# RWKV-7 chain outputs batched over four chunks, pairwise products grouped apart from transposes, low-rank rest weights padded to all rows

## The chip, the cores and the metric

The kernel runs on one core of a Trainium2 chip. The metric is the device time of one execution in microseconds (us). Three runs of the kernel before took 931.61, 930.42 and 931.18 us, with a median of 931.18 us.

## What is computed

One layer of a hybrid block over 512 tokens of width 1024: a norm, one wide input projection, two branches beside each other (RWKV-7 time mixing and a chunked Gated DeltaNet), sigmoid gates that merge them, an output projection, a gated MLP with a causal convolution, and a last norm. The change lies in the RWKV-7 branch, of 8 heads with 64 features:

```python
w_log = -softplus(-(w0 + tanh(wl) @ w2)) - 0.5      # wl, al: 64 wide, low rank
a = sigmoid(a0 + al @ a2)
kk = l2norm(heads(k * k_k)); k = k * (1 + (a - 1) * k_a)
def step(S, inp):                                   # per token and head
    sa = einsum('bhvk,bhk->bhv', S, a_t)
    S = S * w_t + sa * b_t + v_t * k_t              # outer products
    y = einsum('bhvk,bhk->bhv', S, r_t)
    return S, y
```

The kernel computes the scan in 8 chunks of 64 tokens: the state goes from chunk to chunk, and the outputs `y` of a chunk need the state at its start and the solved values inside it.

## The kernel before

Features lie on partitions, the 512 tokens in the free dimension. Nearly all of the work is dense products: a unit of 128 output features takes its weights from memory (`unit`, L148), splits them into two fp32r parts `hi` (ScalarE, L161) and `lo` (VectorE or GpSimd, L163), and multiplies both by the activations in three passes (`mm3`, L169: L176, L177, L179; 24 products of 128x512 for an input unit). The string `ORDER` (L26) is the order in which stages are written; a scheduler then makes one fixed instruction list for each engine from it, in which dense products of later units fill the places where a stage waits. Each engine works through its list strictly in order.

The parts that the change touches:

- `first_tiles` (L256) loads the low-rank weights once and leaves their rest part `ll` in one tile, the decay's in partitions 0 to 63 and the rate's in 64 to 127 (L289, L290). `rwkv_prep` (L422), called once for each of four head pairs (R0 to R3 in `ORDER`), multiplies them: L438 and L474 over all 128 rows of the array, L439 and L475 over 64.
- `rwkv_prep` ends with two halves of four chunks. For each chunk there are two products over 64 rows (L504, L505) and a transpose over all rows (L506), written in turns.
- `rwkv_chain` (L585), called for head pairs 0 and 1 and again for 2 and 3 (c0 and c1 in `ORDER`), runs 8 chunks. A chunk has these steps: L618 and L619 (PE, `128*64`), the copy `Z` (VectorE, L621), L624 (PE, `64*64`), the scaling of the result by VectorE and ScalarE in turns (L626, L627), L630 and L631 (PE, `128*64`), and the new state (VectorE, L637, or L640 in the first chunk), from which the next chunk starts. Beside this loop stand 8 output products a chunk: L642 and L644 (`128*64`), L643 and L645 (`64*64`). ScalarE takes the outputs away once in four chunks (L648).

`128*64`, `64*64`, `64*128` and `128*128` are the array's forms, rows by columns in use, as the profile writes them. A product of fp32 operands is two passes, that is two rows of the profile; a product of fp32r operands is one.

```python
for i, hp in enumerate(hps):
    nc.tensor.matmul(py[lo, i, c4, :], se[:, i, 0, :], R[hp]["ase"][:, c, 1, :], start=True, stop=False)
    nc.tensor.matmul(py[lo, i, c4, :], se[lo, i, 1, :], R[hp]["ntb"][lo, c, 1, :], start=False, stop=True)
    nc.tensor.matmul(py[hi, i, c4, :], so[:, i, 0, :], R[hp]["aso"][:, c, 1, :], start=True, stop=False)
    nc.tensor.matmul(py[hi, i, c4, :], so[hi, i, 1, :], R[hp]["ntb"][hi, c, 1, :], start=False, stop=True)
```

Of the kernel before, what the change touches and what calls it, by code (L numbers as in the profile page):

```python
# [16 lines left out]
T = 512  # L17
# [16 lines left out]
# columns of the per-feature parameter array  # L34
# [9 lines left out]
# columns of the shape-only constant array  # L44
# [49 lines left out]
class Body:  # L94
# [27 lines left out]
    # elementwise work without PSUM operands that GpSimd takes over from VectorE  # L122
# [13 lines left out]
    # work of the second stream takes its temporaries from its own slots  # L136
# [31 lines left out]
    # ps (+)= W^T A with both operands in two parts; act(k) gives the k-th activation tile's parts  # L168
# [35 lines left out]
    # running sum of squares over feature tiles, then 1/sqrt(mean) on all partitions  # L204
# [17 lines left out]
    def run(self):  # L222
# [11 lines left out]
        self.ll = c.tile([128, 512], F32R, name="lora_l")  # L234
# [19 lines left out]
    # the input, its norm, and the first projections, which take the gained but not yet normalised  # L254
    # input and are scaled per token afterwards
    def first_tiles(self, xp):  # L256
# [6 lines left out]
        # zero products keep the array's clock up until the first operands are there  # L263
# [22 lines left out]
        # the low-rank weights stand twice, on either half of the partitions, beside both parts of their input  # L286
        nc.scalar.activation(self.lh, raw, AF.Copy)
        lo, hi = slice(0, 64), slice(64, 128)
        for s, o in ((lo, 0), (hi, 512)):  # L289
            self.on("q").tensor_tensor(out=self.ll[s], in0=raw[s, o:o + 512], in1=self.lh[s, o:o + 512].bitcast(F32), op=ALU.subtract)  # L290
# [48 lines left out]
    # token shift mix of one dense tile  # L339
# [13 lines left out]
    def mixing(self, first):  # L353
# [37 lines left out]
        # the first branch's projection, in the inverse's tiles  # L391
# [7 lines left out]
    # one tile of the branch gates; without a place for it on chip it goes out and comes back for the merge  # L399
# [22 lines left out]
    def rwkv_prep(self, hp, first=None):  # L422
# [12 lines left out]
        # decay  # L435
# [3 lines left out]
        nc.tensor.matmul(ps, self.ll[0:64, fs], self.xw[0:64], start=False, stop=True)  # L439
# [13 lines left out]
        # key norm: one over the squared norm, per token and head on partitions  # L453
# [18 lines left out]
        # in-context rate and replacement key  # L472
        ps = self.bank()
        nc.tensor.matmul(ps, self.lh[:, 512 + hp * 128:640 + hp * 128], self.xa, start=True, stop=False)  # L474
        nc.tensor.matmul(ps, self.ll[64:128, fs], self.xa[64:128], start=False, stop=True)  # L475
# [15 lines left out]
        # bonus  # L491
# [4 lines left out]
        # pairwise products inside a chunk  # L496
        rwm = self.con("rwm")
        for h in range(2):
            pe, po, pt = self.bank(), self.bank(), self.bank()
            for c in range(4):  # L500
                o = slice(c * 128, c * 128 + 128)
                cc = 4 * h + c
                bk = bkh[h][:, c, :, :].rearrange("p s t -> p (s t)")
                nc.tensor.matmul(pe[:, o], bk[0:64], ase[0:64, cc].rearrange("p s t -> p (s t)"), start=True, stop=True)  # L504
                nc.tensor.matmul(po[:, o], bk[64:128], aso[64:128, cc].rearrange("p s t -> p (s t)"), start=True, stop=True)  # L505
                nc.tensor.transpose(pt[:, o], bk, self.con("ident"))  # L506
# [14 lines left out]
    # transposed inverses of G unit triangular 32x32 blocks per 32 partitions, Y = I + N^T Y: a block goes  # L521
    # to J partitions, each with every J-th of its columns
# [62 lines left out]
    def rwkv_chain(self, g, R):  # L585
# [3 lines left out]
        # the values lose their mean over a head's features here: the recurrence is linear in each of  # L589
        # them, so the output that the group norm takes has none either  # L590
        cent = self.con("cent")

        def suv():
            return [self.mp.tile([128, 2, 2, 64], F32, tag=f"SUV{x}", name=self.nm("SUV"), bufs=2) for x in "eo"]
# [3 lines left out]
        nc.gpsimd.memset(so[hi, :, 0, :], 0.0)  # L598
        for c in range(8):
            if c % 4 == 0:  # L600
                pv = self.bank().rearrange("p (c i t) -> p c i t", c=4, i=2)
                py = self.bank().rearrange("p (i c t) -> p i c t", c=4, i=2)
# [5 lines left out]
            c4 = c % 4  # L608
            for tl, s in ((se, hi), (so, lo)):
                nc.scalar.activation(tl[s], pv[s, c4].unsqueeze(2).broadcast_to([64, 2, 2, 64]), AF.Copy)  # L610
            ws = self.mp.tile([128, 2, 64], F32, tag="WS", name=self.nm("WS"), bufs=2)
            if c:
# [28 lines left out]
            for i, hp in enumerate(hps):  # L641
                nc.tensor.matmul(py[lo, i, c4, :], se[:, i, 0, :], R[hp]["ase"][:, c, 1, :], start=True, stop=False)  # L642
                nc.tensor.matmul(py[lo, i, c4, :], se[lo, i, 1, :], R[hp]["ntb"][lo, c, 1, :], start=False, stop=True)  # L643
                nc.tensor.matmul(py[hi, i, c4, :], so[:, i, 0, :], R[hp]["aso"][:, c, 1, :], start=True, stop=False)  # L644
                nc.tensor.matmul(py[hi, i, c4, :], so[hi, i, 1, :], R[hp]["ntb"][hi, c, 1, :], start=False, stop=True)  # L645
            if c4 == 3:
                for i, hp in enumerate(hps):
                    nc.scalar.activation(R[hp]["v"][:, (c - 3) * 64:(c + 1) * 64].rearrange("p (c t) -> p c t", c=4),  # L648
                                         py[:, i], AF.Copy)
# [88 lines left out]
    def gdn_prep(self, h):  # L738
# [6 lines left out]
        # twice the silu of the convolved query, key and value; the norms come in as factors per token:  # L745
        # the key's through beta and the value, the query's through the guard of the output's norm
# [307 lines left out]
```

## Time and profile before

| what | value |
|---|---|
| median of three runs | 931.18 us |
| span of the profiled execution | 929.5 us; what lies around it in the median run is 1.7 us |
| mean granted TensorE clock | 0.993 of full |
| busy: PE, VectorE (DVE), ScalarE (ACT), GpSimd (POOL) | 897.3, 599.5, 466.0, 193.5 us |
| instructions on PE | 4925 matmuls, 4925 weight loads |

A PE row's duration is the time from its start to its modelled end, and one product starts before the one ahead of it has ended. What a product costs is therefore read as the distance from its start to the next start, not as its duration.

### The profile page before, as it was taken

The page shows a single profiled execution, that of the slowest core. Times are in us where ns is not written, and L with a number is a line of the kernel's source. Part 1 is how long each engine was busy: PE and PEld are TensorE (multiplying, and loading weights), DVE is VectorE, ACT ScalarE, POOL GpSimd, SP SyncE. Part 2 cuts the span into 40 slices and gives each one's busy share as a digit, 9 for nine tenths or more (in the row PEclk, how much of TensorE's full clock was granted, in tenths as well). Part 3 has the DMA queues.
Part 4 walks back from the last instruction along what each step waited for, and adds up shares of the span by engine and source line. Part 5 has one row for each costly group of instructions (what it writes and reads, how often), then busy time and mean ns, then how long its engine had stood idle before and what let it go on. Part 6 is the DMA issues. An engine that isn't in the chain of part 4 may idle for free.

```text
span 929.5 us, 13149 instructions
## 1 busy us (share of the span) xinstructions
PE 897.3 (97%) x4925; PEld 686.4 (74%) x4925; DVE 599.5 (65%) x1156; ACT 466.0 (50%) x887; POOL 193.5 (21%) x180
## 2 busy tenths in 40 slices
PE   8999998999999989999999999999999999999995
PEld 5767676665766676666787788888888888888885
DVE  6799797762888995664458445887666666412125
ACT  7744456557643766548533445444444444423233
POOL 1331123101211121101122221222222222222221
PEclk8999999999999999999999999999999999999998
DMA  6422121121112220115343332333322333233334
GB/s 230 136 81 71 57 79 56 47 68 34 59 46 79 68 69 24 57 58 178 106 133 139 95 109 69 109 95 97 106 92 90 95 104 97 80 107 84 104 95 139
DMA packets 28737, 84.76 MB, mean 91 GB/s; under 512 B 3200, under 2 KB 5376, under 8 KB 28672
## 3 DMA queue, kind: packets, MB, share of 16 engines
q1 hardware_dynamic: 28672, 83.91, 28.7%
q8 instruction: 39, 0.64, 0.3%
q14 instruction: 26, 0.21, 0.1%
HBM read 78.13 MB, written 5.77 MB: 90 GB/s over the span
## 4 chain that ended last, share of the span: by engine, by line
PE 75%; DVE 17%; ACT 4%; issue 2%; DMA 1%; POOL 1%; SPq 0%; DVEq 0%; POOLq 0%; ACTq 0%
PE D L179 20%; PE D L176 19%; PE D L177 19%; DVE R L510 2%; PE A L176 1%; PE A L177 1%; PE A L179 1%; DVE P L732 1%; DVE lo L163 1%; DVE invN L539 1%; DVE invY L541 1%; DVE BK L490 1%; DMA raw<-w_in 1%; PE B L643 1%; PE B L644 1%
## 5 line engine op out<-in xcount | busy, mean ns | idle before, releaser
L163 POOL TENSOR_TENSOR lo<-raw,hi 128x512 fp32r<-128x512 f32 x133 | 178.3, 1341 | 662.6 <-ACT hi L161 653.9
L161 ACT ACTIVATE hi<-raw 128x512 fp32r<-128x512 f32 (+1 forms) x266 | 164.7, 621 | 243.1 <-PE D L179 183.1
L176 PE MATMUL D<-uh,lo 128*128 128x512 f32 (+1 forms) x456 | 184.9, 407 | 2.3 <-ACT uh L200 1.9
L177 PE MATMUL D<-uh,hi 128*128 128x512 f32 (+1 forms) x456 | 184.4, 405 | 0.0
L163 DVE TENSOR_TENSOR lo<-raw,hi 128x512 fp32r<-128x512 f32 (+1 forms) x133 | 93.1, 700 | 80.8 <-ACT hi L161 80.3
L179 PE MATMUL D<-ul,hi 128*128 128x512 f32 (+1 forms) x456 | 138.7, 406 | 0.4 <-DVE ul L198 0.4
L176 PE MATMUL D<-u2h,lo 128*128 128x512 f32 x352 | 138.2, 393 | 0.0
L177 PE MATMUL D<-u2h,hi 128*128 128x512 f32 x352 | 138.0, 392 | 0.0
L176 PEld LDWEIGHTS D<-uh,lo 128*128 128x128 f32 x456 | 85.7, 188 | 23.1 <-ACT uh L200 2.4
L177 PEld LDWEIGHTS D<-uh,hi 128*128 128x128 f32 x456 | 85.9, 188 | 18.8 <-issue 1.4
L179 PEld LDWEIGHTS D<-ul,hi 128*128 128x128 f32 x456 | 82.5, 188 | 19.6 <-issue 1.0
L179 PE MATMUL D<-u2l,hi 128*128 128x512 f32 x352 | 94.6, 391 | 0.0
L957 DVE SCALAR_TENSOR_TENSOR P<-T,vecs,P 128x511 f32<-128x511 f32 x88 | 77.4, 880 | 7.4 <-ACT P L955 2.2
L176 PEld LDWEIGHTS D<-u2h,lo 128*128 128x128 f32 x352 | 66.1, 188 | 15.1 <-issue 0.4
L179 PEld LDWEIGHTS D<-u2l,hi 128*128 128x128 f32 x352 | 66.1, 188 | 14.5
L177 PEld LDWEIGHTS D<-u2h,hi 128*128 128x128 f32 x352 | 66.1, 188 | 14.3 <-issue 0.2
L954 DVE TENSOR_TENSOR T<-D,acc 128x512 f32<-128x512 f32 x44 | 30.3, 688 | 41.0 <-PE D L179 37.0
L177 PE MATMUL D<-ah,hi 128*128 128x512 f32 (+1 forms) x126 | 45.2, 366 | 0.0
L176 PE MATMUL D<-ah,lo 128*128 128x512 f32 (+1 forms) x126 | 45.1, 366 | 0.0
L955 ACT ACTIVATE P<-T,vecs 128x512 f32<-128x512 f32 x44 | 31.8, 722 | 8.8 <-DVE T L954 6.0
L539 DVE TENSOR_TENSOR invN<-invA,invY 128x60 f32<-128x60 f32 (+24 forms) x124 | 33.6, 271 | 2.8
L541 DVE TENSOR_TENSOR invY<-invY,invN 128x60 f32<-128x60 f32 (+24 forms) x124 | 33.0, 266 | 2.7
(345 smaller groups left out, 1329.6 us busy)
## 6 DMA issues: line engine op xcount, KB each, us to landing
raw<-w_in SPq DMA_DIRECT2D x44, 512.0 KB, 3.6
raw<-ffn_up SPq DMA_DIRECT2D x44, 512.0 KB, 3.6
raw<-ffn_down SPq DMA_DIRECT2D x18, 512.0 KB, 3.6
raw<-w_out SPq DMA_DIRECT2D x8, 512.0 KB, 3.7
spill<-T SPq DMA_DIRECT2D x14, 256.0 KB, 2.0
R<-spill SPq DMA_DIRECT2D x14, 256.0 KB, 5.3
raw<-ffn_down SPq DMA_DIRECT2D x9, 384.0 KB, 3.1
xin<-xT SPq DMA_DIRECT2D x8, 256.0 KB, 5.4
```

The source lines that it names most:

```text
L161: nc.scalar.activation(hi[:, 0:w], raw[:, o:o + w], AF.Copy)
L163: self.on(str(self.halves % 4)).tensor_tensor(out=lo[:, 0:w], in0=raw[:, o:o + w], in1=hi[:, 0:w].bitcast(F32), op=ALU.subtract)
L176: nc.tensor.matmul(ps, wl[:, w[k]], x[k][0], start=(first and i == 0 and k == 0), stop=False)
L177: nc.tensor.matmul(ps, wh[:, w[k]], x[k][0], start=False, stop=False)
L179: nc.tensor.matmul(ps, wh[:, w[k]], x[k][1], start=False, stop=(last and i == len(parts) - 1 and k == n - 1))
L490: self.on("c").tensor_tensor(out=bkh[h][s, :, sk, :], in0=q(K, s, h), in1=q(em, s, h), op=ALU.mult)
L510: nc.vector.tensor_tensor(out=tl[s, w].rearrange("p c s t -> p c (s t)"), in0=ps[s, :].rearrange("p (c t) -> p c t", c=4), in1=rwm[s].unsq ...
L539: nc.vector.tensor_tensor(out=w, in0=rows[:, t, 0:t].unsqueeze(2).broadcast_to([128, t, n]), in1=Ym[:, t, c:G].unsqueeze(1).broadcast_to([ ...
L541: nc.vector.tensor_tensor(out=Ym[:, 0:t, c:G], in0=Ym[:, 0:t, c:G], in1=w, op=ALU.add)
L954: nc.vector.tensor_tensor(out=h, in0=ps, in1=self.acc2, op=ALU.mult)
L955: nc.scalar.activation(cv, h, AF.Copy, scale=w(2))
L957: nc.vector.scalar_tensor_tensor(out=cv[:, sh:], in0=h[:, 0:T - sh], scalar=w(2 - sh), in1=cv[:, sh:], op0=ALU.mult, op1=ALU.add)
```

## The change

Three edits, and room made for them. The outputs of a chain are no longer issued chunk by chunk: the states of four chunks are kept (`SUV` gets six buffers in place of two), and all outputs of chunks 0 to 3 are issued after chunk 4, those of chunks 4 to 7 after chunk 7; first all 16 products of form `128*64`, then all 16 of form `64*64`, low and high half in turns. In the preparation the four transposes of a half follow its eight products. The low-rank rest weights become two tiles of 128 rows, with zeros in the other half, so that their products use all rows. In the last chunk the scaled state `ws`, which nothing reads there, is no longer made. The scratch for dynamic DMA is set to 1024. The other lines of the diff are removed comments.

```diff
-        self.ll = c.tile([128, 512], F32R, name="lora_l")
+        self.ll = [c.tile([128, 512], F32R, name=f"lora_l{i}") for i in range(2)]
...
-        for s, o in ((lo, 0), (hi, 512)):
-            self.on("q").tensor_tensor(out=self.ll[s], in0=raw[s, o:o + 512], in1=self.lh[s, o:o + 512].bitcast(F32), op=ALU.subtract)
+        for ll, s, z, o in ((self.ll[0], lo, hi, 0), (self.ll[1], hi, lo, 512)):
+            nc.gpsimd.memset(ll[z].bitcast(F32), 0.0)
+            self.on("q").tensor_tensor(out=ll[s], in0=raw[s, o:o + 512], in1=self.lh[s, o:o + 512].bitcast(F32), op=ALU.subtract)
...
-        nc.tensor.matmul(ps, self.ll[0:64, fs], self.xw[0:64], start=False, stop=True)
+        nc.tensor.matmul(ps, self.ll[0][:, fs], self.xw, start=False, stop=True)
...
-        nc.tensor.matmul(ps, self.ll[64:128, fs], self.xa[64:128], start=False, stop=True)
+        nc.tensor.matmul(ps, self.ll[1][:, fs], self.xa, start=False, stop=True)
...
-                nc.tensor.transpose(pt[:, o], bk, self.con("ident"))
+            for c in range(4):
+                nc.tensor.transpose(pt[:, c * 128:c * 128 + 128], bkh[h][:, c, :, :].rearrange("p s t -> p (s t)"), self.con("ident"))
...
+        def outputs(c0, kept):
+            py = self.bank().rearrange("p (i c t) -> p i c t", c=4, i=2)
+            for j, (e, o) in enumerate(kept):
+                for i, hp in enumerate(hps):
+                    for s, tl, a in ((lo, e, "ase"), (hi, o, "aso")):
+                        nc.tensor.matmul(py[s, i, j, :], tl[:, i, 0, :], R[hp][a][:, c0 + j, 1, :],
+                                         start=(j == 0 and i == 0), stop=False, skip_group_check=True)
+            for j, (e, o) in enumerate(kept):
+                for i, hp in enumerate(hps):
+                    for s, tl in ((lo, e), (hi, o)):
+                        nc.tensor.matmul(py[s, i, j, :], tl[s, i, 1, :], R[hp]["ntb"][s, c0 + j, 1, :],
+                                         start=False, stop=True, skip_group_check=True)
+            for i, hp in enumerate(hps):
+                nc.scalar.activation(R[hp]["v"][:, c0 * 64:c0 * 64 + 256].rearrange("p (c t) -> p c t", c=4),
+                                     py[:, i], AF.Copy)
...
+            kept.append((se, so))
...
-            if c:
+            if c and c < 7:
...
+            if c in (4, 7):
+                outputs(c // 4 * 4 if c == 7 else 0, kept[:4])
+                kept = kept[4:]
...
-    nc = bacc.Bacc("TRN2", target_bir_lowering=False, num_devices=1)
+    nc = bacc.Bacc("TRN2", target_bir_lowering=False, num_devices=1, dynamic_dma_scratch_size=1024)
```

In the changed kernel's numbering the loop's PE lines L618, L619, L624, L630, L631 are L639, L640, L645, L651, L652; the `128*64` outputs are L605, the `64*64` outputs L610; L504, L505, L506 are L505, L506, L508.

PE's list in the first chain, the end of chunk 1 (L643 to L645 and L642 are outputs, D rows are dense products, `SUV` holds state and solved values). Before:

```order
L179 MATMUL D_1951<-ul,hi_1943 128x512
L645 MATMUL B_1534<-R_272,SUV_1574 64x64
L642 MATMUL B_1534<-R_564,SUV_1573 64x64
L179 MATMUL D_1951<-ul,hi_1943 128x512
L643 MATMUL B_1534<-R_564,SUV_1573 64x64
L644 MATMUL B_1534<-R_564,SUV_1574 64x64
L179 MATMUL D_1951<-ul,hi_1943 128x512
L630 MATMUL B_1594<-SUV_1573,R_272 64x64
L631 MATMUL B_1594<-SUV_1574,R_272 64x64
L630 MATMUL B_1594<-SUV_1573,R_564 64x64
L631 MATMUL B_1594<-SUV_1574,R_564 64x64
L645 MATMUL B_1534<-R_564,SUV_1574 64x64
```

The same place of PE's list in the changed kernel, the end of chunk 1:

```order
L179 MATMUL D_1948<-ul,hi_1940 128x512 x4
L176 MATMUL D_1948<-uh,lo_1945 128x512
L177 MATMUL D_1948<-uh,hi_1944 128x512
L651 MATMUL B_1587<-SUV_1574,R_275 64x64
L652 MATMUL B_1587<-SUV_1575,R_275 64x64
L651 MATMUL B_1587<-SUV_1574,R_567 64x64
L652 MATMUL B_1587<-SUV_1575,R_567 64x64
L176 MATMUL D_1948<-uh,lo_1945 128x512
L177 MATMUL D_1948<-uh,hi_1944 128x512
L176 MATMUL D_1948<-uh,lo_1945 128x512
L639 MATMUL B_1619<-SUV_1606,R_275 64x64
L640 MATMUL B_1619<-SUV_1607,R_275 64x64
```

Pairs of outputs between single dense products are gone from the chunk; the loop's own groups of four stay, with three dense products between L652 and the next L639.

PE's list in the second head pair's preparation, first half (`BK` and `cons` are operands of the transposes). Before:

```order
L504 MATMUL A_731<-R_564,BK_716 128x128
L505 MATMUL A_732<-R_564,BK_716 128x128
L504 MATMUL A_731<-R_564,BK_716 128x128
L505 MATMUL A_732<-R_564,BK_716 128x128
L506 MATMUL A_733<-cons,BK_716 128x128 x2
L504 MATMUL A_731<-R_564,BK_716 128x128
L505 MATMUL A_732<-R_564,BK_716 128x128
L506 MATMUL A_733<-cons,BK_716 128x128
L504 MATMUL A_731<-R_564,BK_716 128x128
L505 MATMUL A_732<-R_564,BK_716 128x128
L506 MATMUL A_733<-cons,BK_716 128x128
L177 MATMUL D_860<-uh,hi_856 128x512
```

In the changed kernel:

```order
L505 MATMUL A_734<-R_567,BK_719 128x128
L506 MATMUL A_735<-R_567,BK_719 128x128
L505 MATMUL A_734<-R_567,BK_719 128x128
L506 MATMUL A_735<-R_567,BK_719 128x128
L508 MATMUL A_736<-cons,BK_719 128x128 x4
L177 MATMUL D_863<-uh,hi_859 128x512
```

The eight products stand in one piece, and the four transposes behind them.

## Rows read from the trace of the kernel before

**Rows 1.** The page's first part: busy time of an engine, its share of the span, and its instructions.

```profile
PE 897.3 (97%) x4925; PEld 686.4 (74%) x4925; DVE 599.5 (65%) x1156; ACT 466.0 (50%) x887; POOL 193.5 (21%) x180
```

**Rows 2.** Busy time by stretch, in us from the span's start: length, then PE, PEld, DVE, ACT and POOL busy (instructions), the granted clock of PE, the share of the DMA engines and GB/s. The first two are the two chains, the others preparations of head pairs.

```profile
160.00:228.00 68.00, 66.97 (x511) 43.12 (x511) 39.93 (x139) 38.56 (x102) 7.80 (x11) 1.00 0.16 48
349.00:418.00 69.00, 68.66 (x575) 44.72 (x571) 43.41 (x151) 38.44 (x105) 7.97 (x13) 1.00 0.15 47
...
60.00:100.00 40.00, 35.62 (x181) 25.14 (x179) 33.80 (x55) 15.13 (x27) 5.81 (x7) 1.00 0.20 66
260.00:300.00 40.00, 37.79 (x212) 28.11 (x212) 33.31 (x63) 15.77 (x30) 5.92 (x5) 1.00 0.17 53
```

**Rows 3.** The timeline of PE among dense products: start, duration (us), engine, line, operation, form, shape and count of merged instructions.

```profile
79.69 1.09 PE L179 MATMUL D<-ul,hi 128*128 128x512 f32 x4
80.62 0.40 PE L176 MATMUL D<-uh,lo 128*128 128x512 f32 x1
```

**Rows 4.** The timeline of PE in the first chain, outputs of chunk 1 between dense products, with the columns of rows 3.

```profile
176.28 0.40 PE L179 MATMUL D<-ul,hi 128*128 128x512 f32 x1
176.60 0.32 PE L643 MATMUL B<-R,SUV 64*64 64x64 f32 x2
176.86 0.33 PE L644 MATMUL B<-R,SUV 128*64 128x64 f32 x2
177.12 0.50 PE L179 MATMUL D<-ul,hi 128*128 128x512 f32 x1
177.55 0.33 PE L645 MATMUL B<-R,SUV 64*64 64x64 f32 x2
177.80 0.33 PE L642 MATMUL B<-R,SUV 128*64 128x64 f32 x2
178.06 0.50 PE L179 MATMUL D<-ul,hi 128*128 128x512 f32 x1
```

**Rows 5.** The timeline of PE in the first chain, the loop's L618 and L619 (four products, eight passes) between dense products, with the same columns.

```profile
181.54 0.40 PE L176 MATMUL D<-uh,lo 128*128 128x512 f32 x1
181.87 0.27 PE L618 MATMUL B<-SUV,R 128*64 128x64 f32 x1
...
182.25 0.50 PE L177 MATMUL D<-uh,hi 128*128 128x512 f32 x1
182.59 0.39 PE L176 MATMUL D<-uh,lo 128*128 128x512 f32 x1
```

**Rows 6.** The timeline of PE at the first chain's start: the first and last of 32 passes (16 products of form `64*64` on either row half into one PSUM tile), and the dense product behind them.

```profile
160.00 0.27 PE L606 MATMUL B<-cons,R 64*64 64x64 f32 x1
...
160.93 0.22 PE L607 MATMUL B<-cons,R 64*64 64x64 f32 x1
161.08 0.50 PE L176 MATMUL D<-uh,lo 128*128 128x512 f32 x1
```

**Rows 7.** The timeline of PE at a low-rank product (L439 over 64 rows) among products over all rows.

```profile
76.73 0.41 PE L438 MATMUL A<-xw,lora_h 128*128 128x512 f32 x1
77.07 0.50 PE L439 MATMUL A<-xw,lora_l 64*128 64x512 f32 x1
77.50 0.50 PE L179 MATMUL D<-ul,hi 128*128 128x512 f32 x1
77.83 0.39 PE L176 MATMUL D<-uh,lo 128*128 128x512 f32 x1
```

**Rows 8.** The timeline of PE: L624 and L630 of chunk 2, and L624 of chunk 6, in the first chain.

```profile
183.15 0.45 PE L624 MATMUL B<-Z,R 64*64 64x64 f32 x8
...
186.81 0.27 PE L630 MATMUL B<-SUV,R 128*64 128x64 f32 x1
...
213.42 0.45 PE L624 MATMUL B<-Z,R 64*64 64x64 f32 x8
```

**Rows 9.** The timeline of ScalarE at the scalings L627 behind these two L624 (in brackets idle time before, and what ended it).

```profile
183.95 0.31 ACT L627 ACTIVATE SUV<-B,rs 64x64 f32<-64x64 f32 x1 [1.50 <-DVE SUV L626]
184.60 0.31 ACT L627 ACTIVATE SUV<-B,rs 64x64 f32<-64x64 f32 x1 [0.34 <-DVE SUV L626]
...
214.28 0.31 ACT L627 ACTIVATE SUV<-B,rs 64x64 f32<-64x64 f32 x1
...
215.53 0.62 ACT L161 ACTIVATE hi<-raw 128x512 fp32r<-128x512 f32 x1
216.17 0.31 ACT L627 ACTIVATE SUV<-B,rs 64x64 f32<-64x64 f32 x1
```

**Rows 10.** The timeline at a new state in the first chain (chunk 3): the last pass of L630 on PE, and the four updates L637 on VectorE.

```profile
194.94 0.22 PE L630 MATMUL B<-SUV,R 128*64 128x64 f32 x1
...
195.29 1.23 DVE L637 SCALAR_TENSOR_TENSOR SUV<-B,wc,WS 64x64 f32<-64x64 f32 x4 [1.64 <-PE B L631]
```

**Rows 11.** Who waited for whom over the whole span: us in total, times, longest.

```profile
PE A L494 <- DVE P L492: 4.4, 4, 1.6
...
PE B L624 <- DVE Z L621: 0.5, 1, 0.5
...
ACT hi L161 <- PE D L179: 183.1, 124, 3.7
PE D L176 <- POOL lo L163: 1.5, 2, 0.8
```

More of the change, by code (lines that the diff above doesn't have):

```diff
@@ L593, in suv @@
         def suv():
-            return [self.mp.tile([128, 2, 2, 64], F32, tag=f"SUV{x}", name=self.nm("SUV"), bufs=2) for x in "eo"]
+            return [self.mp.tile([128, 2, 2, 64], F32, tag=f"SUV{x}", name=self.nm("SUV"), bufs=6) for x in "eo"]
+        def outputs(c0, kept):
[13 more added lines that the diff above has]
+                                     py[:, i], AF.Copy)
         se, so = suv()
@@ L598, in rwkv_chain @@
         nc.gpsimd.memset(so[hi, :, 0, :], 0.0)
+        kept = []
         for c in range(8):
@@ L601, in rwkv_chain @@
                 pv = self.bank().rearrange("p (c i t) -> p c i t", c=4, i=2)
-                py = self.bank().rearrange("p (i c t) -> p i c t", c=4, i=2)
                 for c2 in range(4):
@@ L608, in rwkv_chain @@
             c4 = c % 4
+            kept.append((se, so))
             for tl, s in ((se, hi), (so, lo)):
                 nc.scalar.activation(tl[s], pv[s, c4].unsqueeze(2).broadcast_to([64, 2, 2, 64]), AF.Copy)
-            ws = self.mp.tile([128, 2, 64], F32, tag="WS", name=self.nm("WS"), bufs=2)
-            if c:
+            if c and c < 7:
+                ws = self.mp.tile([128, 2, 64], F32, tag="WS", name=self.nm("WS"), bufs=2)
                 for i, hp in enumerate(hps):
@@ L640, in rwkv_chain @@
                             nc.vector.tensor_scalar_mul(tl[s, i, 0, :], pz[s, 2, i, :], w)
[L641 to L649, printed above, removed]
+            if c in (4, 7):
+                outputs(c // 4 * 4 if c == 7 else 0, kept[:4])
+                kept = kept[4:]
             if c < 7:
```

## The prediction

> **What bounds the kernel now.** I read the page's busy times first. PE is busy for 97% of the span, VectorE for 65%, ScalarE for 50% [rows 1]. A busy PE need not be a PE at its best pace, so I then took stretches. In the two chains PE is busy for 66.97 of 68 us and 68.66 of 69 us, at a granted clock of 1.00, while VectorE works for 39.93 and 43.41 us [rows 2]. PE's list is the bound there, and what leaves it shortens the stretch, as long as no other wait comes up. In the preparations it is less clear: PE stands idle for 4.4 of 40 us (60 to 100) and for 2.2 of 40 us (260 to 300), with VectorE near 33.5 us of 40 [rows 2]; the longest waits for VectorE are at L494, 4.4 us in four times [rows 11]. What PE saves there may turn into waiting.
>
> Last I read the distances between PE's starts. Four dense products take 0.93 us, 0.233 us each [rows 3]. Where the array's form changes the distances grow. From the dense product at 177.12 to the one at 178.06 are 0.94 us; in them lie one dense product (0.233), two outputs and three changes of form [rows 4]. A product inside a long run of its own form costs 0.93 / 16 = 0.058 us [rows 6]. So three changes cost 0.94 - 0.233 - 0.116 = 0.59 us, **0.20 us each**. Two other places say the same: two dense products and four L618/L619 products take 1.05 us from 181.54 to 182.59, which leaves 0.35 us for two changes, 0.18 each [rows 5]; three 512-column products with a low-rank one among them take 1.10 us, which leaves 0.40 for two [rows 7].
>
> **The change part by part.** The number of products is the same, 4086 in both lists; what differs is how often neighbours have another form. I counted this through both lists. Before there are 365 changes of form, after it 204. In the chains 286 become 155; changes to or from `64*128` (products and low-rank) go from 46 to 16.
>
> *Outputs in batches.* 131 changes fewer by 0.20 us give **26.2 us**; by 0.18 us, 23.6. The 128 outputs were 128 pieces of their own; now they are 19 pieces, and inside a piece a product costs 0.058 us. The extra cost of a lone output is already in the 0.20, since that price was taken from lone outputs [rows 4].
>
> *New waits in the chains.* This is what the gain is paid with. The outputs also filled time in which PE would have waited for the loop's next step, and dense products must now do it alone. Three handovers per chunk, with what they need and what the new list puts between, by the prices above:
>
> - From L624 to L630 (L645 to L651 after), over the scalings. From L624 at 183.15 to the end of the last scaling (184.60 + 0.31) are 1.76 us, while PE came to L630 only after 3.66; where a weight split stood in ScalarE's list between the two scalings it was 3.06 us (213.42 to 216.48) [rows 8, 9]. The new list has between 1.86 and 4.11 us of PE work there in the 14 chunks that need it, and 2.43 or less in five of them. With a need of 1.76 nothing waits; with 2.4 it sums to 1.2 us, with 3.06 to 5.8 us.
> - From L631 to the next L618 (L652 to L639). The first two of four updates are done some 0.97 us after the last pass of L630 (194.94, then 195.29 plus half of 1.23) [rows 10]. The new list covers about 1.05 us in nearly every chunk. That is enough, unless something else stands in VectorE's list: 0 to 8 us over 14 chunks, if nothing or half a microsecond does.
> - From L619 to L624, over the copy `Z`. It made PE wait once, 0.5 us [rows 11]. Four chunks are covered tightly: 0.6 us.
>
> Together 0 to 14.4 us. I take **6 us**, since most chunks have cover but no longer much of it.
>
> *Preparation.* 30 changes fewer by 0.20 us are 6.0 us on PE: 16 of them at the eight low-rank products, 14 at products and transposes. Where PE waits for VectorE anyway this is given back, so the bounds are 0 and 6; I take **3 us**. A product with the padded rows is one more 512-column product in the same form; its price of 0.233 us holds, and its weights are made once.
>
> *Edits with one answer.* The two fills of 64x512 stand at the head of GpSimd's list, which is empty there; if they delayed the first splits, the price would show at L176's wait for GpSimd, 1.5 us in all now [rows 11]. The four scalings `ws` of chunk 7 leave ScalarE, which is at 56% in the chains [rows 2]: nothing. The list of DMAs keeps its number of transfers, and a smaller scratch moves none. The outputs' copies by ScalarE come one chunk later, and the branch's end only has to be ready for the projection far behind it. The scheduler also reordered the first two projections; I put that at 0, within 1.5 us to either side by the same wait [rows 11].
>
> *Sum.* 26.2 - 6 + 3 = 23.2 us. The profiled execution has a span of 929.5 us and the median of the runs is 931.18, 1.7 us around it that the change doesn't touch. 931.2 - 23.2 = **908 us**.
>
> **The rivals.**
>
> *PE was the only bound.* No handover waits, and the preparations keep all that PE saves: 26.2 + 6.0 = 32.2 us, 899 us. For it speaks that PE almost never waits for the loop now. Against it: the cover at L652 to L639 falls to a tenth of a microsecond above the need. Chance 0.20.
>
> *The loop's handovers bind.* Waits at their upper end, 14.4 us, changes at 0.18 us and nothing from the preparations: 23.6 - 14.4 = 9.2 us, 922 us. VectorE's 40 us of work in a chain would then have to fit in some 60 us with in-order waits on PE. Chance 0.12.
>
> *The second half of a batch runs one by one.* The 64 outputs of form `64*64` come from both row halves of the array and go to one PSUM tile. If the two halves could not write there side by side, each product would keep the distance of a lone one, about 0.26 us [rows 4], in place of 0.058: 64 x 0.2 = 12.8 us less, 921 us. L606 and L607 speak against it: either row half, one PSUM tile, and still 0.058 us each [rows 6]. The Trainium skill (TensorEngine Tiling (Array Packing), Restrictions and Gotchas) says that different row tiles cannot access the same PSUM bank at a time; by that rule this rival would be the forecast, and the rows just named differ from it for halves that write different partitions. Chance 0.03.
>
> *Slower: ScalarE's list holds the loop up.* A weight split L161 waits for the dense products that still read its buffer, 183.1 us in all and up to 3.7 us at once [rows 11], and ScalarE works strictly in order. If a split stands ahead of the second scaling, its wait comes into the handover to L651. The new list has a split between the two scalings in five of 16 chunks, the old one in three. It decides when the 14 handovers lose more than (26.2 + 3) / 14 = 2.1 us each; with 3.7 us at each the kernel would take 931.2 - 29.2 + 51.8 = 954 us. Chance 0.02.
>
> *The change doesn't do what it says.* The scheduler could have spread the outputs again. The lists exclude it: 19 pieces in place of 128.
>
> **How the numbers follow.** The forecast, 903 to 915 us around 908, has 0.63, the rivals 0.20, 0.12, 0.03 and 0.02. The likeliest case gives the time. The range reaches from PE as the only bound to the side of binding handovers, 899 to 920 us, and leaves out the ends of both. A measurement of this kernel tells 0.2%, or 1.9 us, from no change. Only the last rival is slower, and a chain that gives nearly all back would be needed for no change: faster 0.96, same 0.02, slower 0.02.
>
> **What would show it.** In the profile after, the chains from the first centring product to L676 should take some 58 us in place of 68, with batches of 32 products in about 2.1 us each. PE should wait at L651 and L639, where it waited for almost nothing before, some 6 us in all. A low-rank product should stand 0.23 us from its neighbours. The dense part behind the projections should keep its length, and the granted clock stay at 1.00. I am wrong if outputs inside a batch stand at 0.25 us, if L651 and L639 wait for over 12 us, or if the time saved in the chains comes back as idle time behind them, at the second inverse or in the preparations.

## The result, and the profile after

The changed kernel took 900.47 us (median of 4 runs, 899.88 to 901.19) beside 931.39 us for the kernel before on the same chip (930.42 to 931.70): 0.9672 of its time, 95% interval 0.9658 to 0.9685, or 30.9 us less. The profiled execution took 901.19 us with a span of 899.4 us; the span before was 929.5 us.

The first part of the page after answers to [rows 1]. PE is still the busiest engine, with 31.1 us less busy time and the same number of instructions:

```profile
PE 866.2 (96%) x4925; PEld 675.9 (75%) x4925; DVE 590.1 (66%) x1156; ACT 464.0 (52%) x879; POOL 195.4 (22%) x182
```

Stretches of the changed kernel, with the columns of [rows 2]: the two chains, then the two preparations.

```profile
157.00:214.00 57.00, 56.17 (x518) 38.75 (x516) 39.17 (x142) 36.40 (x98) 7.77 (x12) 1.00 0.18 57
331.00:388.00 57.00, 55.10 (x576) 39.29 (x575) 43.97 (x150) 37.32 (x102) 8.36 (x13) 1.00 0.15 48
60.00:100.00 40.00, 36.59 (x198) 27.34 (x197) 35.41 (x61) 15.64 (x27) 6.41 (x8) 0.96 0.23 75
257.00:297.00 40.00, 37.95 (x212) 28.55 (x210) 35.79 (x88) 17.19 (x30) 5.88 (x5) 1.00 0.19 63
```

The chains have the same work in some 57 us, at full clock. PE idles 0.8 and 1.9 us in them, against 1.0 and 0.3 us in [rows 2]: the new order asks for few waits.

PE's timeline at the first chain's first batch, with the columns of [rows 3]:

```profile
189.85 0.57 PE L605 MATMUL B<-R,SUV 128*64 128x64 f32 x13
190.45 0.45 PE L645 MATMUL B<-Z,R 64*64 64x64 f32 x8
190.83 0.80 PE L605 MATMUL B<-R,SUV 128*64 128x64 f32 x18
191.56 1.15 PE L610 MATMUL B<-R,SUV 64*64 64x64 f32 x32
192.64 0.49 PE L176 MATMUL D<-uh,lo 128*128 128x512 f32 x1
```

The 32 passes of L610, 16 products, take 1.08 us from start to next start, one change of form included: (1.08 - 0.20) / 16 = 0.055 us each, as L606 and L607 in [rows 6], where a lone output had cost 0.26 us [rows 4].

A low-rank product (L440) among its neighbours, answering to [rows 7]: the distances are 0.26 and 0.23 us.

```profile
77.28 0.42 PE L439 MATMUL A<-xw,lora_h 128*128 128x512 f32 x1
77.54 0.39 PE L440 MATMUL A<-xw,lora_l 128*128 128x512 f32 x1
77.77 0.40 PE L179 MATMUL D<-ul,hi 128*128 128x512 f32 x1
```

Who waited for whom over the whole span, answering to [rows 11] (PEld is the weight load, which runs ahead of the product):

```profile
ACT hi L161 <- PE D L179: 193.5, 138, 2.4
PEld B L651 <- ACT SUV L648: 5.7, 11, 1.0
PEld B L639 <- DVE SUV L658: 4.6, 14, 0.4
PE A L495 <- DVE P L493: 3.2, 3, 1.9
PE D L176 <- POOL lo L163: 1.3, 1, 1.3
PE B L651 <- ACT SUV L648: 1.5, 3, 0.7
...
DVE R L512 <- PE A L506: 1.1, 4, 0.4
```

PE itself waits 1.5 us at L651; at L639 its weight load does, mostly at most 0.4 us at a time, and PE for 0.2 us in all.

Where the 30 us of span went is read from the starts of landmark rows; L690/L705 is the first product of the other branch's gates, L661/L676 the first product behind a chain, L993/L1008 the first sum of the last norm (line before/line after). Beside each stage stand the 512-column products and form changes between the same places of PE's list; a product more costs 0.233 us [rows 3].

| stage | before us (products, changes) | after us (products, changes) | difference |
|---|---|---|---|
| start to first low-rank product | 46.3 (158, 0) | 47.4 (158, 0) | +1.2 |
| to the first product L504/L505 | 23.6 (77, 4) | 23.5 (77, 0) | 0 |
| to L690/L705 | 35.9 (92, 18) | 33.0 (90, 8) | -2.8 |
| to the first chain | 54.3 (169, 10) | 53.8 (171, 10) | -0.5 |
| first chain, to L661/L676 | 67.8 (121, 137) | 56.2 (123, 75) | -11.6 |
| to the last L504/L505 | 62.8 (156, 31) | 59.4 (154, 17) | -3.3 |
| to the second chain | 58.1 (173, 4) | 57.9 (173, 4) | -0.3 |
| second chain, to L661/L676 | 69.4 (109, 149) | 56.9 (104, 80) | -12.5 |
| to the last norm's L993/L1008 | 491.5 (2014, 12) | 491.6 (2019, 10) | +0.1 |

The rest, 19.8 us before and 19.7 after, is the end. With the products that moved between stages taken out, the chains give 12.1 + 11.4 = 23.5 us for 131 changes, the stages of preparation, that is the rows to the first chain and those between the two chains, 6.5 us. The start took 45.2 to 47.4 us in all the profiles of this study, without regard to the edit, so its 1.2 us is not put down to the change.

### The profile page after: what moved, and what is told of

Read it like the earlier page. It is cut to its first block, busy times and chain, and to the rows that moved or that the text cites. A ratio compares the mean times of both kernels' runs of the same rounds, so it can differ in the third digit from the quotient of the medians.

```text
span 899.4 us, 13124 instructions
## 1 busy us (share of the span) xinstructions
PE 866.2 (96%) x4925; PEld 675.9 (75%) x4925; DVE 590.1 (66%) x1156; ACT 464.0 (52%) x879; POOL 195.4 (22%) x182
## 4 chain that ended last, share of the span: by engine, by line
PE 73%; DVE 16%; ACT 4%; issue 3%; DMA 2%; POOL 1%; SPq 0%; DVEq 0%; POOLq 0%; ACTq 0%
PE D L179 20%; PE D L176 20%; PE D L177 20%; DVE R L512 1%; PE A L176 1%; PE A L177 1%; PE A L179 1%; DVE invN L541 1%; DVE lo L163 1%; DVE P L747 1%; DMA raw<-w_in 1%; DVE invY L543 1%; ACT hi L161 1%; DVE R L926 1%; PE B L639 1%
## 5 line engine op out<-in xcount | busy, mean ns | idle before, releaser
L161 ACT ACTIVATE hi<-raw 128x512 fp32r<-128x512 f32 (+1 forms) x266 | 165.0, 622 | 257.3 <-PE D L179 193.5
L179 PE MATMUL D<-ul,hi 128*128 128x512 f32 (+1 forms) x456 | 135.4, 403 | 0.4 <-DVE ul L198 0.4
L176 PEld LDWEIGHTS D<-uh,lo 128*128 128x128 f32 x456 | 86.2, 189 | 23.5 <-ACT uh L200 2.4
L179 PEld LDWEIGHTS D<-ul,hi 128*128 128x128 f32 x456 | 82.6, 188 | 19.6 <-issue 1.2
L179 PE MATMUL D<-u2l,hi 128*128 128x512 f32 x352 | 95.1, 392 | 0.0
L179 PEld LDWEIGHTS D<-u2l,hi 128*128 128x128 f32 x352 | 66.1, 188 | 14.1
L972 DVE SCALAR_TENSOR_TENSOR P<-T,vecs,P 128x511 f32<-128x511 f32 x88 | 69.0, 784 | 8.9 <-ACT P L970 2.8
L177 PE MATMUL D<-ah,hi 128*128 128x512 f32 (+1 forms) x126 | 45.2, 366 | 0.0
```

The costliest lines, as they stand in the source:

```text
L161: nc.scalar.activation(hi[:, 0:w], raw[:, o:o + w], AF.Copy)
L176: nc.tensor.matmul(ps, wl[:, w[k]], x[k][0], start=(first and i == 0 and k == 0), stop=False)
L177: nc.tensor.matmul(ps, wh[:, w[k]], x[k][0], start=False, stop=False)
L179: nc.tensor.matmul(ps, wh[:, w[k]], x[k][1], start=False, stop=(last and i == len(parts) - 1 and k == n - 1))
L972: nc.vector.scalar_tensor_tensor(out=cv[:, sh:], in0=h[:, 0:T - sh], scalar=w(2 - sh), in1=cv[:, sh:], op0=ALU.mult, op1=ALU.add)
```

## The experiments

Each ran beside the kernel before; those of one group share its runs, with medians of 931.52 (e1 to e4), 931.07 (e5 to e8) and 931.10 us (e9 to e12).

**The three edits apart: e1, e2, e3.** Each is the kernel before with one of the diff's parts: e1 the low-rank weights, e2 the transposes behind the products, e3 the outputs with their buffers and scratch.

```diff
...
-        nc.tensor.matmul(ps, self.ll[0:64, fs], self.xw[0:64], start=False, stop=True)
+        nc.tensor.matmul(ps, self.ll[0][:, fs], self.xw, start=False, stop=True)
...
-        nc.tensor.matmul(ps, self.ll[64:128, fs], self.xa[64:128], start=False, stop=True)
+        nc.tensor.matmul(ps, self.ll[1][:, fs], self.xa, start=False, stop=True)
...
```

> The kernel before with the low-rank edit alone (two rest tiles of 128 rows with zeros, and the smaller scratch that the room for them needs). PE's list has 351 changes of array form in place of 365. Theory 1 (each change of form costs PE 0.20 us, and PE is the bound): up to 14 x 0.20 = 2.8 us less, 928.6 us; L440 stands 0.23 us from its neighbours. Theory 2 (the gain comes from the outputs' new place in time and from the PSUM tile and state buffers that they free, not from forms): 931.4 us, no change. If this edit also causes the first 1.4 us that the changed kernel loses ahead of its first low-rank product, the first L439 starts at 47.7 us in place of 46.3 and the gain is 1.4 us.

```diff
-                nc.tensor.transpose(pt[:, o], bk, self.con("ident"))
+            for c in range(4):
+                nc.tensor.transpose(pt[:, c * 128:c * 128 + 128], bkh[h][:, c, :, :].rearrange("p s t -> p (s t)"), self.con("ident"))
```

> The kernel before with the transposes of a half behind its products, and nothing else. 351 changes of form in place of 365. Theory 1: 14 x 0.20 = 2.8 us less, 928.6 us; if PE there waits for VectorE anyway, between 0 and 2.8. Theory 2: 931.4 us.

```diff
...
+            kept.append((se, so))
...
+            if c in (4, 7):
+                outputs(c // 4 * 4 if c == 7 else 0, kept[:4])
+                kept = kept[4:]
...
```

> The kernel before with the batched outputs alone (and the six state buffers and the scratch that they need). 232 changes of form in place of 365. Theory 1: 133 x 0.20 = 26.6 us less, less some 2 us of new waits: 907 us; with the two other edits' 28 changes, 5.6 us, it makes up the changed kernel's 30.9. Theory 2: nearly all of the gain, 901 to 903 us.

e1: 931.5 us, ratio 1.0006 (0.9994 to 1.0017), no gain. e2: 926.04 us, 0.9943 (0.9931 to 0.9955), 5.4 us less. e3: 907.1 us, 0.9743 (0.9730 to 0.9755), 24.4 us less. The outputs do what their changes of form are worth; 5.4 + 24.4 = 29.8 of the whole's 30.9 us. The other two miss in opposite directions, and their rows tell how.

In e1, PE comes sooner to the next product that waits for ScalarE. PE's timeline before, then that of e1 (in brackets idle time before and what ended it):

```profile
84.11 1.05 PE L459 MATMUL A<-cons,T 128*128 128x2 f32 x8 [0.77 <-ACT T L455]
```

```profile
83.00 1.05 PE L460 MATMUL A<-cons,T 128*128 128x2 f32 x8 [1.14 <-ACT T L456]
...
84.73 0.63 PE L179 MATMUL D<-ul,hi 128*128 128x512 f32 x1
85.16 0.63 PE L176 MATMUL D<-uh,lo 128*128 128x512 f32 x1
```

The wait grows by 0.37 us, nearly the 0.40 us that the product before it had saved. An earlier wait, for VectorE, takes back as much; PE's timeline before and in the whole change (e1 has 1.86 us there):

```profile
68.76 1.12 PE L494 MATMUL A<-P,cons 128*128 128x512 f32 x2 [1.47 <-DVE P L492]
```

```profile
69.89 1.13 PE L495 MATMUL A<-P,cons 128*128 128x512 f32 x2 [1.85 <-DVE P L493]
```

In e1, behind the longer wait before L460, dense products stand 0.43 us apart in place of 0.233, which is the clock's lower level, 1.2 GHz; from 80 to 90 us the granted clock was 0.83 in e1 and in the whole change, 1.00 in the kernel before, e2, e3 and e12.

In e2 it is VectorE that gains. Its masks L510 (L511 in e2) of the last products, in VectorE's timeline, and its waits over the whole span; first before, then e2:

```profile
75.73 2.71 DVE L510 TENSOR_TENSOR R<-A,cons 64x512 f32<-64x512 f32 x4 [1.06 <-PE A L505]
```

```profile
DVE R L510 <- PE A L505: 5.9, 4, 1.6
```

```profile
74.16 2.71 DVE L511 TENSOR_TENSOR R<-A,cons 64x512 f32<-64x512 f32 x4 [0.18 <-PE A L505]
```

```profile
DVE R L511 <- PE A L505: 1.2, 4, 0.4
```

VectorE waits 4.7 us less for the products, which no longer have transposes among them; the stages to L690 and to the last L504 are 2.4 us shorter each, 4.7 in all. The wait is 5.9 us in e1 and e3 as well, and 1.1 us in the whole change.

**The same batches in turns of form: e4.** The products also get back the `start` and `stop` flags that they had in the kernel before.

```diff
                     for s, tl, a in ((lo, e, "ase"), (hi, o, "aso")):
-                        nc.tensor.matmul(py[s, i, j, :], tl[:, i, 0, :], R[hp][a][:, c0 + j, 1, :],
-                                         start=(j == 0 and i == 0), stop=False, skip_group_check=True)
-            for j, (e, o) in enumerate(kept):
-                for i, hp in enumerate(hps):
-                    for s, tl in ((lo, e), (hi, o)):
-                        nc.tensor.matmul(py[s, i, j, :], tl[s, i, 1, :], R[hp]["ntb"][s, c0 + j, 1, :],
-                                         start=False, stop=True, skip_group_check=True)
+                        nc.tensor.matmul(py[s, i, j, :], tl[:, i, 0, :], R[hp][a][:, c0 + j, 1, :], start=True, stop=False)
+                        nc.tensor.matmul(py[s, i, j, :], tl[s, i, 1, :], R[hp]["ntb"][s, c0 + j, 1, :], start=False, stop=True)
```

> The changed kernel, with the outputs of a batch written in the order of the kernel before: 128*64, 64*64, 128*64, 64*64 for each chunk and head pair. The batches, their place in the list, the kept states and the PSUM tiles are those of the changed kernel; 311 changes of form in place of 204. Theory 1: 107 x 0.20 = 21.4 us more, 921.9 us, and outputs 0.26 us apart inside a batch. Theory 2: the gain stays, 900 to 905 us.

It took 940.8 us, 1.0096 (1.0080 to 1.0111): slower than before, which no theory expected. That theory 2 falls is plain. The chains took 76.5 and 77.1 us, 20.3 and 20.2 more than after, for 54 and 53 changes more (10.8 and 10.6 us). The other 19 us are put down to the clock, which shows in PE's timeline in the first batch:

```profile
193.60 0.33 PE L605 MATMUL B<-R,SUV 128*64 128x64 f32 x2
193.86 0.33 PE L606 MATMUL B<-R,SUV 64*64 64x64 f32 x2
194.12 0.47 PE L605 MATMUL B<-R,SUV 128*64 128x64 f32 x2
194.52 0.47 PE L606 MATMUL B<-R,SUV 64*64 64x64 f32 x2
...
201.71 0.63 PE L176 MATMUL D<-uh,lo 128*128 128x512 f32 x1
202.13 0.63 PE L177 MATMUL D<-uh,hi 128*128 128x512 f32 x1
```

The same stretches of e4, with the columns of [rows 2]:

```profile
170.00:180.00 10.00, 10.00 (x63) 6.77 (x64) 7.28 (x29) 5.13 (x13) 1.29 (x1) 1.00 0.18 53
190.00:200.00 10.00, 10.00 (x69) 7.31 (x67) 2.68 (x12) 0.95 (x4) 0.00 (x0) 0.70 0.19 59
200.00:210.00 10.00, 10.00 (x39) 6.13 (x40) 4.54 (x19) 4.13 (x12) 0.84 (x1) 0.50 0.00 0
```

After a string of outputs 0.256 us apart, the distance goes to 0.40 us, and dense products behind it stand 0.42 us apart. The clock fell to its lower level while PE's row shows no idle time. The price of a change is not that of adding to the place in PSUM just written: in e4 L606 adds to what L605 has just written, in [rows 4] L644 follows L643 and writes the other half, and both stand 0.26 us apart.

**Two chunks a batch: e10 in turns of form, e11 grouped.** These were run to separate the price from the clock. Both copy two chunks' outputs at a time; e10 also has e4's order inside its batches.

```diff
...
-            if c in (4, 7):
-                outputs(c // 4 * 4 if c == 7 else 0, kept[:4])
-                kept = kept[4:]
+            if c in (2, 4, 6, 7):
+                outputs(6 if c == 7 else c - 2, kept[:2])
+                kept = kept[2:]
```

> The kernel after with batches of two chunks in place of four, and inside a batch the two forms in turns, product by product; 302 form changes; unbroken strings of outputs are at most 12 products long in place of up to 26. Theory 1 (0.20 us per form change, and the further 19 us of the four-chunk batches in turns came from the lower clock): with the clock at 1.00 in the chains, 900.5 + (302 - 204) x 0.20 = 920.1 us, within 2.5. Rival (outputs in turns cost more than 0.20 per change, whatever the clock, or the clock falls as well in the shorter strings): 930 us or more, with the granted clock at 0.9 or less in the chains in the second case.

> The kernel after with batches of two chunks in place of four, grouped by form as in it; 195 form changes. Theory 1: 9 x 0.20 = 1.8 us less than after, 898.7 us, less what the handovers cost if the smaller batches cover them less well: 898 to 901 us; the distance to the same batches in turns of form is (302 - 195) x 0.20 = 21.4 us. Rival (four chunks are needed, since the piece of 32 products is what gains): about half of the 24.4 us of the outputs is lost, 910 us or more.

e10 took 925.22 us, 0.9943 (0.9923 to 0.9962); e11 901.7 us, 0.9684 (0.9669 to 0.9698), no different from the whole change. Between them lie 23.5 us for 107 changes, 0.22 us each with what the lower clock cost e10. Strings half as long lower the clock less, but still do. The first batches' stretch, e10 and then e11:

```profile
190.00:200.00 10.00, 10.00 (x70) 6.59 (x68) 4.78 (x21) 3.61 (x12) 0.42 (x1) 0.83 0.01 2
```

```profile
190.00:200.00 10.00, 9.97 (x92) 6.59 (x92) 7.30 (x32) 7.47 (x21) 1.60 (x2) 1.00 0.24 82
```

So e10's 5 us above theory 1 go with the clock, though its share was not measured apart, and the rival that the clock falls in shorter strings too holds in part. A batch of two chunks is enough.

**Halves, room, and smaller groups: e5, e6, e7.** e5 changes only the order inside the changed kernel's batches; e6 gives the kernel before the buffers and the scratch of the change; e7 groups the eight outputs of each chunk by form in the kernel before.

```diff
-            for j, (e, o) in enumerate(kept):
-                for i, hp in enumerate(hps):
-                    for s, tl, a in ((lo, e, "ase"), (hi, o, "aso")):
+            for s, x, a in ((lo, 0, "ase"), (hi, 1, "aso")):
+                for j, eo in enumerate(kept):
+                    for i, hp in enumerate(hps):
```

> The kernel after, but inside a batch the 8 products of the low half stand together and then the 8 of the high half, in both forms; the form changes stay at 204. Theory 1 (a change of the array's form costs 0.20 us, and neighbours of one form cost 0.058 us each whichever halves they use): the batches keep 32 passes in about 1.1 us per form, 900.5 us, within 1.5. Rival (the gain came from low and high half running side by side, since each uses half of the array's columns): neighbours that use the same half must go one by one, at about 0.11 us each in place of 0.057 if each only runs alone (+0.055 x 128 = 7 us, 907 us), at 0.256 us each if each drains the array like the lone outputs of before (128 x 0.2 = +25 us, 926 us).

```diff
-            return [self.mp.tile([128, 2, 2, 64], F32, tag=f"SUV{x}", name=self.nm("SUV"), bufs=2) for x in "eo"]
+            return [self.mp.tile([128, 2, 2, 64], F32, tag=f"SUV{x}", name=self.nm("SUV"), bufs=6) for x in "eo"]
...
```

> The kernel before with six SUV buffers in place of two and a dynamic DMA scratch of 1024, nothing else; 365 form changes as before. Theory 1 (the order of forms is the gain): 931.4 us, no difference beyond 0.2%. Rival (the room alone, that is SUV buffers coming free sooner for the scalings, gave part of the 24 us of the outputs): some us below 931, up to 907.

```diff
-                nc.tensor.matmul(py[lo, i, c4, :], se[:, i, 0, :], R[hp]["ase"][:, c, 1, :], start=True, stop=False)
...
+                for s, tl, a in ((lo, se, "ase"), (hi, so, "aso")):
+                    nc.tensor.matmul(py[s, i, c4, :], tl[:, i, 0, :], R[hp][a][:, c, 1, :],
+                                     start=(c4 == 0 and i == 0), stop=False, skip_group_check=True)
+            for i, hp in enumerate(hps):
+                for s, tl in ((lo, se), (hi, so)):
+                    nc.tensor.matmul(py[s, i, c4, :], tl[s, i, 1, :], R[hp]["ntb"][s, c, 1, :],
+                                     start=False, stop=True, skip_group_check=True)
```

> The kernel before, its outputs still issued chunk by chunk with two buffers, but in each chunk the four outputs of form 128*64 ahead of the four of form 64*64 in the program; the scheduler's list then has 326 form changes, 39 fewer than before. Theory 1: 39 x 0.20 = 7.8 us less, 923.6 us, within 2. Rival (the batch over four chunks is what matters, because the loop's own groups are no longer broken up by outputs): a group of four inside a chunk gains little, 929 to 932 us.

e5 took 906.54 us, 0.9733 (0.9714 to 0.9753), 6.1 us more than the whole change: theory 1, with one price for any neighbour of the same form, falls, and the rival's smaller number (907) is met. Not all of it comes by the rival's way: in the profiles the chains are 4.5 us longer, and 1.8 us lie in the dense part, where the granted clock was 0.90 from 480 to 490 us in e5 and 1.00 in the whole change. L610 in e5's timeline:

```profile
191.78 1.90 PE L610 MATMUL B<-R,SUV 64*64 64x64 f32 x32
193.60 0.49 PE L176 MATMUL D<-uh,lo 128*128 128x512 f32 x1
```

The same 32 passes take 1.82 us in place of 1.08, so a product 0.10 us in place of 0.055. What a product costs that has the array to itself is read from PE's timeline of the whole change, at two fp32 products (four passes) with 512 columns:

```profile
388.18 1.88 PE L676 MATMUL B<-T,cons 128*128 128x512 f32 x4
389.89 1.02 PE L687 MATMUL B<-sg,g 128*128 128x512 f32 x2
```

These are 1.71 us for two, or 0.107 us for 64 columns. With the halves apart the outputs go at about that pace, one by one; low and high half in turns go at twice that pace, so they run side by side, though both write one PSUM tile. The Trainium skill (TensorEngine Tiling (Array Packing), Restrictions and Gotchas) says that different row tiles cannot use the same PSUM bank at once; by that rule the order would not matter, and here 1.08 against 1.82 us speak against it for halves that write different partitions.

e6 took 930.89 us, 0.9999 (0.9986 to 1.0012): the room alone is worth nothing. e7 took 923.43 us, 0.9925 (0.9907 to 0.9944): 7.6 us for 39 changes, as theory 1 had it (7.8).

**Transposes ahead, and the whole without the low-rank edit: e9, e12.**

```diff
             pe, po, pt = self.bank(), self.bank(), self.bank()
+            for c in range(4):
+                nc.tensor.transpose(pt[:, c * 128:c * 128 + 128], bkh[h][:, c, :, :].rearrange("p s t -> p (s t)"), self.con("ident"))
             for c in range(4):
...
-                nc.tensor.transpose(pt[:, o], bk, self.con("ident"))
```

> The kernel before with one edit in the preparation: the four transposes of a half stand ahead of its eight products in place of between them; 343 form changes in place of 365. Theory A (the preparation's edit gains through PE's form changes alone): 22 x 0.20 = 4.4 us less, 927 us, like the run with the transposes behind the products (926.0). Theory B (the preparation is bound by VectorE, and the edit gained 5.4 us because the masks could start sooner, the transposes no longer standing ahead of the last products): here all four transposes stand ahead of every product, so the masks start hardly sooner than before, and PE's saving turns into waiting for VectorE: 930 to 931.5 us.

e12 is the changed kernel with e1's lines as they were before.

> The kernel after without its edit of the low-rank weights; 218 form changes in place of 204. Theory A (PE's form changes add up wherever they stand): 14 x 0.20 = 2.8 us more, 903.3 us. Theory B (around the low-rank products VectorE is the bound, so the edit is given back there, as when it stood alone on the kernel before): 900.5 us, within 1.

e9 took 933.68 us, 1.0026 (1.0011 to 1.0042), outside both theories, and its median decides nothing: the scheduler also moved 18 dense products from the dense part to places before and in the second chain, new waits came up there, and the granted clock was 0.83 from 330 to 340 us, where the kernel before has 1.00. The stages to L690 and to the last L504 were 1.8 and 2.0 us shorter, so theory B's "hardly sooner" is wrong there. Waits of e9 over the whole span:

```profile
DVE R L511 <- PE A L506: 3.1, 3, 1.0
PE A L772 <- POOL T L769: 2.6, 2, 2.2
DVE R L511 <- PE A L507: 0.5, 1, 0.5
```

VectorE's wait at the masks is 3.6 us, between the 5.9 before and the 1.2 of e2, and the two stages' gain of 3.7 us lies below e2's 4.7. By these waits, as an estimate, half of what VectorE gains in e2 comes of the changes alone (5.9 to 3.6 us) and half of the transposes' place behind the products (3.6 to 1.2). For the time e9 does not separate the two.

e12 took 901.93 us, 0.9684 (0.9667 to 0.9701). Its interval overlaps the whole change's and takes in both theories' numbers; with e1 it says that the low-rank edit is worth between nothing and some 2 us. In the profiles' stages of preparation it is worth 0.9 us on top of the others. The granted clock blurs the rest: e12's runs at a mean clock of 0.992, that of the whole change, took 902.7 and 903.2 us, those at 0.994 and 0.995 901.2 and 899.7, and four runs do not settle what the edit is worth at an equal clock.

**One step further: e8.** In each chunk the first head pair's state products are made twice as wide, so that they need both head pairs' states and all four products issue together; nobody reads the added columns.

```diff
+                if i == 0:
+                    nc.tensor.matmul(pz[lo, 0::3, 0, :], R[hp]["ase"][:, c, 0, :], se[:, :, 0, :], start=True, stop=True)
+                    nc.tensor.matmul(pz[hi, 0::3, 0, :], R[hp]["aso"][:, c, 0, :], so[:, :, 0, :], start=True, stop=True)
+                    continue
```

> The kernel after, and in the chains' loop the products of the old state (L639, L640) of both head pairs' new-state input issue together: per half one product over 2 x 64 state columns in place of two in turn, so that form changes go from 204 to 160. Theory 1: 44 x 0.20 = 8.8 us less, 32 wider products cost at most 0.058 us more each (1.9 us): 893.6 us. Rival (the handover over the state's update binds once the first product needs both head pairs' states: two updates of VectorE more, about 0.6 us, before 14 products per chain pair): up to 14 x 0.6 = 8.4 us of waits at L639, 900 to 902 us, no gain.

It took 901.54 us, 0.9688 (0.9673 to 0.9703): no gain, as the rival said. Waits of PE in e8 over the whole span (L655, L640 and L649 are the changed kernel's L651, L639 and L645):

```profile
PE B L655 <- ACT SUV L652: 3.0, 5, 0.8
PE B L640 <- DVE SUV L665: 1.9, 2, 1.4
PE B L649 <- DVE Z L646: 0.8, 1, 0.8
PE B L640 <- DVE SUV L662: 0.4, 2, 0.2
```

They sum to 6.1 us where the whole change has 1.7. The two chains took 54.6 and 57.0 us, 1.5 us less in all, where 6.9 were expected: 4.4 us went into waits, at all three handovers and not at L640 alone. Outside the chains the stage to L705 and the dense part took 1.7 and 1.6 us more. There the clock was lower at other times than in the whole change, as the columns of [rows 2] show, e8 and then the whole change:

```profile
70.00:80.00 10.00, 10.00 (x61) 7.85 (x58) 8.63 (x13) 3.99 (x8) 1.51 (x1) 0.88 0.17 52
480.00:490.00 10.00, 8.75 (x31) 6.99 (x32) 3.36 (x5) 3.66 (x6) 2.57 (x2) 0.83 0.32 107
```

```profile
70.00:80.00 10.00, 9.74 (x65) 7.05 (x66) 9.15 (x15) 4.75 (x9) 0.75 (x1) 1.00 0.18 52
480.00:490.00 10.00, 8.07 (x35) 6.21 (x34) 4.81 (x8) 3.85 (x7) 2.58 (x2) 1.00 0.35 107
```

No version beat the changed kernel.

## Why the prediction was right, and where its sum was off

The time fell 7.5 us below the predicted 908. It lies inside the range, but below the 903 to 915 us of the likeliest case and near the number of the first rival (899): the range held because it reached that far. The terms:

- **Price of a change of form, 0.20 us: right.** e7 gives 7.6 us for 39 changes, e3 24.4 us for 133 less its new waits; e10 against e11 gives 0.22 us each with the lower clock in it. That the order of forms and not the room made the gain is shown by e6, and by e4 and e10, which kept place and buffers. The distance of 0.058 us inside a piece holds only with the halves in turns (e5), which the prediction didn't ask about.
- **New waits in the chains, 6 us: too large.** The chains gave 23.5 of 26.2 us, so 2.7 us were lost; PE's own waits at L651 and L639 are 1.7 us. At L651 the sum came out near the working with a need of 2.4 us (1.2 us of waits), not near that with 3.06 (5.8). The thin cover at L639, for which the sum left room up to 8 us, sufficed: the weight load waits 14 times, 4.6 us, and PE hardly. The mechanism was there all the same: e8 made the handovers longer, and they took the gain.
- **Preparation, 3 us: too small, and by another way than its step had it.** 6.5 us came, more than the bound of 6. The step let PE save time and give half of it back. In fact the low-rank half of the changes (14 by e1's list, not 16) came to nothing alone, while the transposes' half gave 5.4 us (e2), twice its 14 x 0.20 us, with 4.7 us less of VectorE's waits. How much of the 5.4 us is the price and how much the order in which VectorE gets its input was not separated (e9).
- **Edits with one answer: 0, right within a microsecond** as far as could be told; the start's 1.2 us lies inside what it varied by. The dense part kept its length (491.5 and 491.6 us). In other profiles with about as many products it took 491.4 to 491.9 us where the granted clock stayed at 1.00 in it (e1, e3, e4, e6), and 493.0 to 493.8 us where it fell once, between 480 and 510 us (e2, e5, e8, e10, e11, e12).
- **The rivals.** *PE was the only bound* had the right number partly for the wrong reason: the low-rank changes gave little (e1, e12), and VectorE's gain made up for it. *The second half of a batch runs one by one* fell in the batch's rows. *ScalarE's list holds the loop up* did not come: L161's longest wait for L179 is 2.4 us, and PE waited at L651 for 0.7 us at most.
- **What was to be seen.** Chains of some 58 us: 56.2 and 56.9. Batches of about 2.1 us: the first took 2.4 us, with L645 in between. Low-rank neighbours at 0.23 us: 0.23 and 0.26. Waits of some 6 us: 1.7. Clock at 1.00: so in the chains, but 0.83 from 80 to 90 us.

Two errors of the same sign, 3.3 and 3.5 us, thus make most of the 7.5 us.

## What to carry to other kernels

Where PE is the bound and small products of several array forms are mixed, count the changes of form in its list and price them from the distance between starts; group the products by form, with low and high half in turns, even if only two loop steps fit in a batch. Before adding a saving on one engine to the sum, follow it to the next wait of that engine (e1), and look also at who gets its input sooner (e2). A handover that has slack now may have none after the next regrouping (e8).

## What the runs showed of the hardware

Unbroken strings of lone small products lowered TensorE's clock although its row is busy throughout: in e4 the granted clock was 1.00 from 170 to 180 us, 0.70 from 190 to 200 and 0.50 from 200 to 210, and by the working above it cost some 19 us. The Trainium skill (TensorE: Matmul & The Clock Gate, The HAM clock gate) calls the lower level that of an idle engine; by that reading e4 would have kept 1.00 in those stretches, and the trace differs. The second case is two waits that the low-rank edit lengthens, before L495 (1.47 to 1.85 us) and before L460 (0.77 to 1.14 us). All seven profiles with this edit ran for some us at the lower level behind one of them: e1, e4, e5 and the whole change behind the second (0.83 from 80 to 90 us), e8 and e10 behind the first (0.88 and 0.85 from 70 to 80 us), e11 behind both. The seven without it had 1.00 from 60 to 100 us. What decides behind which wait the clock falls stays open.
